# Retention projections of a hybrid decoder: seven products of quarter sums in place of eight

## The chip, the cores and the metric

The kernel runs on one core of a Trainium2 chip. The metric is the device time of one execution in microseconds (us). The kernel before took 1365.76 us, the median of two runs (1365.38 and 1366.14).

## The reference, cut to what matters

The model is a decoder trunk of four sub-layers on x of 512 tokens by 1024 features, float32: retention, a gated feed-forward block (ffn) with a short convolution, stick-breaking attention, and a second ffn. Each normalises its input and adds its output to x. Only the retention is changed:

```python
def _retention(h, w_in, w_out):              # h = rmsnorm(x, ret_norm), (B, S, D)
    proj = h @ w_in
    q, k, v, g = jnp.split(proj, [RET_QK, 2 * RET_QK, 2 * RET_QK + RET_V], axis=-1)
    ...                                       # rotary on q and k, per head
    scores = jnp.einsum('bhncd,bhnkd->bhnck', qc, kc) * dmat[None, :, None]
    intra = jnp.einsum('bhnck,bhnke->bhnce', scores, vc)
    ...                                       # a decayed state carries earlier blocks
    o = intra + jnp.moveaxis(cross, 0, 2)
    o = o * lax.rsqrt(jnp.mean(o * o, axis=-1, keepdims=True) + EPS)
    y = jax.nn.silu(g.astype(jnp.float32)) * o
    return y.astype(h.dtype) @ w_out
```

There are four heads; q and k have 256 columns a head, v and g 512. So a head has 512 columns of q and k, 512 of v, 512 of g, and 512 rows of the output projection.

## The kernel before

x lies feature-major in SBUF, eight tiles `x[0..7]` of 128 features by 512 tokens. A float32 product is made as three matmuls: each operand is split into a rounded high part and a low part (`split`, `parts`), and `mm3` (L137 to L139) issues high x high, high x low and low x high into one PSUM accumulator. x is split once as `xh`, `xl` (gain applied, but not the row factor r of the normalisation); weights arrive as chunks of 128x1024 (512 KB) through `chunk` (L122): SP issues the load into a `raw` buffer, ScalarE casts it to `hi` (L130), VectorE subtracts to get `lo` (L131). raw, hi and lo have five buffers each.

r is known only when all squares are summed (`rsqrt`, L216 to L220). It is applied late: to cos and sin, by which q and k are multiplied on their way out of PSUM (`rope`, L263 to L268); to v as a per-token scale (L111, L112, L304); to g by a multiplication on the way out (L367).

The retention goes head by head. `first4` computes q and k of head 0 while x is loaded. Each further projection step of a head (q and k, v, g) takes 96 matmuls of 512 columns, as does the output projection. `ret_scores` and `ret_av` are the causal attention with a fixed decay; `ret_av` keeps its four sums in PSUM until they are multiplied by their row factor (L357). PSUM has eight banks: four `att`, three `acc`, one `one`. The projections of heads 1 to 3 and all of g go through `acc`, attention through `att`. The output projection of head h-1 stands after v of head h, those of heads 2 and 3 at the end.

The order on each engine comes from the framework's planner: it takes the program's order as priority and its own estimate of when operands are ready, and lays out a fixed queue for each engine. So a later projection may be placed between the matmuls of attention.

In the ffn, four parts of the down projection are already made by seven products in place of eight (`fast_down`): both operands are cut into quarters, seven products of sums of quarters are made, and their results are added and subtracted into x. The sums of activations are made on VectorE (L434 to L436), the sums of weights by DMA from DRAM to DRAM on POOL's queue, with accumulation (`weight_sums`, L516, L518): 64 of them, started by an instruction on POOL (L500) that waits for r. Each sum needs up to six DMAs one after another, and two halves go side by side.

Of the kernel before, what the change touches and what calls it, by code (L numbers as in the profile page):

```python
# [9 lines left out]
F32 = mybir.dt.float32  # L10
F32R = mybir.dt.float32r
# [4 lines left out]
P = 128  # L16
# [15 lines left out]
HALF = S // 2  # L32
WARM = 4
# [3 lines left out]
class Kernel:  # L37
# [12 lines left out]
    def __init__(self, ctx, tc, t):  # L50
# [7 lines left out]
        self.pp = None  # L58
        self.att_pool()
        self.phase("ret")  # L60

# [4 lines left out]
    def phase(self, which):  # L66

        if self.pp is not None:
            self.pp.__exit__(None, None, None)
            self.pp = None  # L70
        if which:
            self.pp = self.tc.tile_pool(name=self.name(which), bufs=1, reuse_waits="tile")
            self.ph = self.pp.__enter__()

# [8 lines left out]
    BUFS = {"xh": 8, "xl": 8, "tt": 8, "rr": 2}  # L83
    PHASE = {"qk": 8, "vv": 8, "yy": 16, "pp": 8, "cs": 4, "ar": 2, "oh": 5, "ol": 5, "sq": 2, "sk": 4, "hl": 1, "bt": 2, "at": 2, "oo": 8}

    def sb(self, tag, cols=S, dt=F32):
        pool, bufs = (self.ap, self.BUFS) if tag in self.BUFS else (self.ph, self.PHASE)
        return pool.tile([P, cols], dt, tag=tag, bufs=bufs[tag], name=self.name(tag))

# [25 lines left out]
    def raw(self):  # L115
        return self.wp.tile([P, CH], F32, tag="raw", bufs=5, name=self.name("raw"))

    def chunk(self, c, cols=CH):

        nc = self.nc  # L120
        raw = self.raw()
        nc.sync.dma_start(raw[:, :cols], c)  # L122
        return self.parts(raw, cols)

    def parts(self, raw, cols=CH):
        nc = self.nc
        hi = self.wp.tile([P, CH], F32R, tag="hi", bufs=5, name=self.name("hi"))
        lo = self.wp.tile([P, CH], F32R, tag="lo", bufs=5, name=self.name("lo"))
        raw, hi, lo = raw[:, :cols], hi[:, :cols], lo[:, :cols]
# [15 lines left out]
    def first4(self, name, load=False):  # L145
# [3 lines left out]
        for k in range(KD):  # L149
            w = self.wchunk(name, k, S)  # L150
            if load:
                self.nc.sync.dma_start(self.x[k], self.t["xT"][k])
                self.norm_split(k, 0)
# [21 lines left out]
    def out_proj_steps(self, name, base, ys, last):  # L175

        n = len(ys)
        for c in range(4):
            w = self.wchunk(name, base + c, n * 256)
            for mm in range(2):  # L180
                ps = self.acc()
                for k in range(n):
                    s = slice(k * 256 + mm * P, k * 256 + mm * P + P)
                    self.mm3(ps, (w[0][:, s], w[1][:, s]), ys[k], k == 0, k == n - 1)
                    yield
                self.add_to_x(2 * c + mm, ps, last)

# [7 lines left out]
    def norm_split(self, m, which):  # L195
# [3 lines left out]
        self.xs.append(self.split(self.x[m], ("xh", "xl"), scale=g))  # L199
# [60 lines left out]
    def rope(self, p1, p2, tail):  # L260
        nc = self.nc
        a, b, e, f = (self.sb("tt") for _ in range(4))
        nc.vector.tensor_mul(a, p1, self.cos)  # L263
        nc.vector.tensor_mul(e, p1, self.sin)
        nc.vector.tensor_mul(b, p2, self.sin)
        nc.vector.tensor_mul(f, p2, self.cos)
# [7 lines left out]
    def ret_qk(self, h, ps):  # L274

        tail = self.sb("vv")
        tail = [tail[:, i * P : (i + 1) * P] for i in range(4)]
        out = []
        for i in range(2):
            c = 4 * (h - 1) + 2 * i  # L280
            x = ps[2 * i : 2 * i + 2] or [self.proj(self.wchunk("rqk", c + j), self.xs) for j in range(2)]
            out.append(self.rope(*x, tail[2 * i : 2 * i + 2]))
        return *out, tail

    def token_major(self, name, base):

        w = [self.wchunk(name, base + c) for c in range(4)]
        for i in range(NT):
# [5 lines left out]
            yield i, ps  # L294

    def ret_v(self, h):
        out = []
        for i, ps in self.token_major("rv", 4 * h):
            rc = self.rc[:, i : i + 1]
            if i < NT - 1:  # L300
                out.append(self.split(ps, ("vv", "vv"), scale=rc))
            else:
                out.append([self.sb("vv")])
                self.nc.scalar.activation(out[i][0], ps, AF.Copy, scale=rc)  # L304
        return out

    def ret_scores(self, h, q, k, tail):
        nc = self.nc
        dec = self.sb("cs", S + P)
# [24 lines left out]
    def ret_av(self, h, v, p):  # L334
# [3 lines left out]
        for m in range(4):  # L338
# [7 lines left out]
            os.append(o)  # L346
# [513 lines left out]
```

## Time and profile before

| what | value |
|---|---|
| median of two runs | 1365.76 us |
| profiled execution | 1366.12 us, span 1363.8 us |
| TensorE matmul busy | 1350.7 us, 99% of the span |
| VectorE, ScalarE busy | 991.1 us (73%), 599.0 us (44%) |
| DMA, mean over the span | 134 GB/s |

The profile is of one execution. The span runs from its first to its last instruction, and the execution's own time is 2.3 us more. A matmul's duration in the trace reaches over its successors, so what one costs is read from the distance between starts. "Busy" of the other engines is close to the time they can't be used by anybody else. The feed-forward's first matmul starts at 401.88 us, which is where the retention ends for TensorE.

### The profile page before, as it was taken

How to read it: one execution, taken by the hardware profiler on the slowest of the kernel's cores; microseconds unless marked ns; L12 is line 12 of the kernel's file. 1: busy time of each engine (PE TensorE's matmuls, PEld its weight loads, DVE VectorE, ACT ScalarE, POOL GpSimd, SP SyncE). 2: the span in 40 equal slices, each digit the busy share in tenths (PEclk: the TensorE clock that was granted, in tenths of full speed). 3: DMA queues.
4: the chain of work that ended last, by engine and by line, in shares of the span. 5: the costliest groups of instructions: out<-in, count | busy, mean ns of one | idle time of the engine just before them, and what ended most of it. 6: DMA issues, size and time to landing. Idle time of an engine off the chain costs nothing.

```text
span 1363.8 us, 18143 instructions
## 1 busy us (share of the span) xinstructions
PE 1350.7 (99%) x7016; PEld 1147.6 (84%) x7016; DVE 991.1 (73%) x1384; ACT 599.0 (44%) x844; POOL 78.3 (6%) x142
## 2 busy tenths in 40 slices
PE   9999999999999999999999999999999999999997
PEld 7888888888888889888988898787788899899887
DVE  7774564564768878688666668879799886787665
ACT  6443333333346444344344454444265443444434
POOL 1222220000000000000000021111000000000000
PEclk9999999999999999999999999999999999999999
DMA  8999992132224335433521574544143345235121
GB/s 299 305 290 243 301 239 96 47 108 77 62 77 141 99 102 169 126 93 107 183 82 55 165 183 124 130 118 109 39 145 95 108 127 168 77 113 174 55 70 62
DMA packets 58308, 182.77 MB, mean 134 GB/s; under 512 B 7024, under 2 KB 9200, under 8 KB 58224
## 3 DMA queue, kind: packets, MB, share of 16 engines
q1 hardware_dynamic: 42880, 136.25, 32.0%
q0 software_dynamic: 13824, 44.05, 13.3%
q10 hardware_dynamic: 1520, 1.33, 0.3%
q8 instruction: 55, 0.90, 0.3%
q14 instruction: 29, 0.24, 0.1%
HBM read 166.92 MB, written 33.55 MB: 147 GB/s over the span
## 4 chain that ended last, share of the span: by engine, by line
PE 95%; DVE 4%; issue 0%; ACT 0%; DVEq 0%; ACTq 0%
PE acc L138 23%; PE acc L137 23%; PE acc L139 23%; PE x L455 6%; PE att L137 4%; PE att L138 4%; PE att L139 4%; PE z L455 3%; PE acc L455 2%; PE one L626 1%; PE z L598 1%; DVE sg L603 1%; PE tp L618 1%; DVE at L620 1%; DVE bt L607 1%
## 5 line engine op out<-in xcount | busy, mean ns | idle before, releaser
L130 ACT CAST hi<-raw 128x1024 fp32r<-128x1024 f32 (+2 forms) x277 | 268.4, 969 | 428.8 <-PE acc L138 290.5
L138 PE MATMUL acc<-xl,hi 128*128 128x512 f32 x992 | 386.8, 390 | 0.0
L137 PE MATMUL acc<-xh,hi 128*128 128x512 f32 x992 | 386.5, 390 | 0.0
L139 PE MATMUL acc<-xh,lo 128*128 128x512 f32 x992 | 386.5, 390 | 0.0
L131 DVE TENSOR_TENSOR lo<-raw,hi 128x1024 fp32r<-128x1024 f32 (+2 forms) x277 | 309.3, 1118 | 61.3 <-ACT hi L130 59.6
L139 PEld LDWEIGHTS acc<-xh,lo 128*128 128x128 f32 x992 | 186.2, 188 | 38.5
L137 PEld LDWEIGHTS acc<-xh,hi 128*128 128x128 f32 x992 | 186.3, 188 | 38.1 <-DVE x L189 0.4
L138 PEld LDWEIGHTS acc<-xl,hi 128*128 128x128 f32 x992 | 186.3, 188 | 37.5 <-issue 0.2
L407 DVE SCALAR_TENSOR_TENSOR tt<-tt,vec,tt 128x511 f32<-128x511 f32 (+1 forms) x176 | 131.3, 747 | 4.0 <-ACT tt L405 1.4
L404 DVE TENSOR_TENSOR tt<-acc,rr 128x512 f32<-128x512 f32 x80 | 55.1, 688 | 75.6 <-PE acc L139 75.6
L189 DVE TENSOR_TENSOR x<-x,acc 128x512 f32<-128x512 f32 x72 | 48.9, 685 | 52.5 <-PE acc L139 52.4
L139 PE MATMUL acc<-hi,xl 128*128 128x512 f32 (+1 forms) x256 | 86.0, 336 | 0.0
L138 PE MATMUL acc<-lo,xh 128*128 128x512 f32 (+1 forms) x256 | 85.9, 336 | 0.0
L137 PE MATMUL acc<-hi,xh 128*128 128x512 f32 (+1 forms) x256 | 85.9, 336 | 0.0
L405 ACT ACTIVATE tt<-tt,vec 128x512 f32<-128x512 f32 x88 | 71.4, 812 | 11.3 <-DVE tt L404 10.2
L455 PE MATMUL x<-oh,hi 128*128 128x256 f32 x240 | 68.2, 284 | 0.0
L455 PE MATMUL x<-oh,lo 128*128 128x256 f32 x240 | 67.9, 283 | 0.0
L455 PE MATMUL x<-ol,hi 128*128 128x256 f32 x240 | 67.9, 283 | 0.0
L603 DVE TENSOR_TENSOR_SCAN sg<-sg,diag 128x512 f32<-128x512 f32 (+3 forms) x64 | 52.3, 818 | 2.0 <-ACT sg L600 1.2
L137 PEld LDWEIGHTS acc<-hi,xh 128*128 128x128 f32 x256 | 48.4, 189 | 5.3
L138 PEld LDWEIGHTS acc<-lo,xh 128*128 128x128 f32 x256 | 48.4, 189 | 5.3
L139 PEld LDWEIGHTS acc<-hi,xl 128*128 128x128 f32 x256 | 48.5, 189 | 4.9
(178 smaller groups left out, 2228.3 us busy)
## 6 DMA issues: line engine op xcount, KB each, us to landing
raw<-in_up SPq DMA_DIRECT2D x80, 512.0 KB, 4.1
sum<-in_fast POOLq DMA_DIRECT2D x36, 512.0 KB, 8.9
raw<-sum SPq DMA_DIRECT2D x24, 512.0 KB, 3.4
raw<-in_fast SPq DMA_DIRECT2D x18, 512.0 KB, 3.6
raw<-in_rv SPq DMA_DIRECT2D x16, 512.0 KB, 6.5
raw<-in_rg SPq DMA_DIRECT2D x16, 512.0 KB, 4.4
raw<-in_rout SPq DMA_DIRECT2D x16, 512.0 KB, 4.8
sk<-hl POOLq DMA_DIRECT2D x32, 256.0 KB, 4.4
```

The lines of the kernel that those rows point to most:

```text
L130: nc.scalar.copy(hi, raw)
L131: nc.vector.tensor_sub(lo, raw, hi.bitcast(F32))
L137: mm(out, a[0], b[0], start=start, stop=False)
L138: mm(out, a[0], b[1], start=False, stop=False)
L139: mm(out, a[1], b[0], start=False, stop=stop)
L189: self.nc.vector.tensor_add(self.x[m], self.x[m], ps)
L404: nc.vector.tensor_mul(u, ps, self.r)
L405: nc.scalar.activation(c, u, AF.Identity, scale=w[2], bias=w[3])
L407: nc.vector.scalar_tensor_tensor(c[:, i:], u[:, : S - i], w[2 - i], c[:, i:], op0=ALU.mult, op1=ALU.add)
L455: mm(out[:, :Q], a[ai], b[bi], start=start and k + i == 0, stop=k == nk - 1 and i == 2, skip_group_check=not start)
L598: nc.tensor.matmul(z[:, :nz], q[:, i * P : (i + 1) * P], k[:, :nz], start=m == 0, stop=m == 1)
L603: nc.vector.tensor_tensor_scan(sg[:, :n][:, ::-1], sg[:, :n][:, ::-1], self.diag[:, S - n :][:, ::-1], 0.0, op0=ALU.mult, op1=ALU.max,)
```

## The change

All of g, q and k of heads 1 to 3, and v of heads 1 to 3 are made by seven products in place of eight. q and k of head 0 (`first4`), v of head 0 (`ret_v0`), attention and the output projection keep their matmuls.

New operands: `ret_operands` makes, from x, gain and r, the normalised x and four sums of its quarters (features in pairs of tiles, tokens in halves), and splits them: four pairs `xo` of 128x1792. It stands after v of head 0. The sums of weights come from DMAs as in the ffn, in the order of `ORDER`: 10 new groups of eight DMAs, one chunk wide except the pair for v of heads 1 and 2, ahead of the ffn's. What starts them is now the last tile of x. The list of seven products is shared (`seven`); `feature_rows` makes feature-major results with 256 token columns a matmul (q and k, g, ffn), `token_rows` token-major ones for v, with 512 weight columns for heads 1 and 2 together and 256 for head 3.

A feature product uses the four `att` banks and two of `acc`; its results are gathered from PSUM into SBUF by ScalarE copies (first) and VectorE additions (later). `ret_av` copies its sums out of PSUM to SBUF. In the retention raw has three buffers, hi and lo four; after it each has five as before. The order of the steps is written out, with parts of the output projection between.

```diff
+ORDER = (
+    ("fg", 0, 1), ("fqk", 0, 1), ("fv", 0, 2), ("fg", 1, 1), ("fqk", 1, 1), ("fg", 2, 1), ("fqk", 2, 1),
+    ("fv3", 0, 1), ("fg", 3, 1), *((f"fast{l}_{s}", 0, 2) for l in range(2) for s in range(FAST[l])),
+)
...
-    BUFS = {"xh": 8, "xl": 8, "tt": 8, "rr": 2}
-    PHASE = {"qk": 8, "vv": 8, "yy": 16, "pp": 8, "cs": 4, "ar": 2, "oh": 5, "ol": 5, "sq": 2, "sk": 4, "hl": 1, "bt": 2, "at": 2, "oo": 8}
+    BUFS = {"tt": 8, "rr": 2}
+    OPERANDS = {"xh": 8, "xl": 8, "xo": 8}
+    PHASE = {"qk": 8, "vv": 6, "vr": 4, "tl": 1, "yy": 12, "pp": 7, "tr": 2, "dc": 1, "ar": 2, "oh": 5, "ol": 5,
+             "sq": 2, "sk": 4, "hl": 1, "bt": 2, "at": 2, "oo": 8, "sv": 8}
...
+    RING = {"raw": (3, 2), "hi": (4, 1), "lo": (4, 1)}
+    def ring(self, tag, dt):
+        a, b = self.RING[tag]
+        i = self.tiles[tag]
+        self.tiles[tag] = (i + 1) % (a if self.now == "ret" else a + b)
+        pool, tag, n = (self.wp, tag, a) if i < a else (self.ph, tag + "+", b)
+        return pool.tile([P, CH], dt, tag=tag, bufs=n, name=self.name(tag[:3]))
...
+    def seven(self, name, i, product, add, x, z, n=1):
+        w = [[self.t[name][c][q] for c in range(i, i + n)] for q in range(4)]
+        s1, s2, s3, s4 = ([self.sums[name][c][q] for c in range(i, i + n)] for q in range(4))
+        product(x, w[0], self.X11, True)
+        add(0, 0, x, 1, True)
+        product(z, s1, self.T1, True)
+        add(1, 1, z, -1, True)
+        product(x, s2, self.T2, False)
+        add(0, 1, x, 1, True)
+        y = [self.acc() for _ in range(2)]
+        product(y, w[1], self.X21, True)
+        add(0, 0, y, 1, False)
+        product(x, s3, self.T3, False)
+        add(1, 1, x, -1, False)
+        product(z, s4, self.X22, False)
+        add(0, 1, z, 1, False)
+        product(x, w[3], self.T4, False)
+        add(1, 0, x, -1, True)
+    def feature_rows(self, name, i, ops, x, z, add):
+        cols = 2 * len(ops) * P
+        def product(to, w, n, start):
+            w = self.chunk(w[0], cols)
+            for p in range(2):
+                self.quarter(to[p], w, p, ops, n, start)
+        self.seven(name, i, product, add, x, z)
+    def feature_tiles(self, name, i):
+        nc = self.nc
+        out = [self.sb("tt") for _ in range(4)]
+        def add(row, half, of, sign, first):
+            for p in range(2):
+                to = out[2 * p + row][:, half * Q : half * Q + Q]
+                if first:
+                    nc.scalar.activation(to, of[p][:, :Q], AF.Copy, scale=float(sign))
+                else:
+                    (nc.vector.tensor_add if sign > 0 else nc.vector.tensor_sub)(to, to, of[p][:, :Q])
+        x, z = ([self.att() for _ in range(2)] for _ in range(2))
+        self.feature_rows(name, i, self.ops, x, z, add)
+        return out
+    def token_rows(self, name, i, n, cols, out):
+        nc = self.nc
+        def product(to, w, q, start):
+            for c, chunk in enumerate(w):
+                w = self.chunk(chunk)
+                nk = CH // cols
+                for a in range(2):
+                    for k in range(nk):
+                        o = slice(q * Q + a * P, q * Q + a * P + P)
+                        op, b = [x[:, o] for x in self.ops[c * nk + k]], [x[:, k * cols : (k + 1) * cols] for x in w]
+                        for j, (ai, bi) in enumerate(((0, 0), (0, 1), (1, 0))):
+                            nc.tensor.matmul(
+                                to[a][:, :cols], op[ai], b[bi], start=start and c + k + j == 0,
+                                stop=c == n - 1 and k == nk - 1 and j == 2, skip_group_check=not start,
+                            )
+        def add(row, half, of, sign, first):
+            for a in range(2):
+                to, ps = out[row][2 * half + a], of[a][:, :cols]
+                if first:
+                    nc.scalar.activation(to, ps, AF.Copy, scale=float(sign))
+                else:
+                    (nc.vector.tensor_add if sign > 0 else nc.vector.tensor_sub)(to, to, ps)
+        x, z = ([self.att() for _ in range(2)] for _ in range(2))
+        self.seven(name, i, product, add, x, z, n)
+    def weight_sums(self):
+        nc, tc, t = self.nc, self.tc, self.t
+        self.sums = {n: {} for n in SUMS}
+        gate = nc.gpsimd.tensor_copy(self.gate, self.x[KD - 1][:, :1])
+        with tc.issue_after(getattr(gate, "ins", gate)):
+            for name, first, n in ORDER:
+                w, cs = t[name], range(first, first + n)
+                cols = w.shape[3]
+                d = {
+                    c: [
+                        self.dp.tile([P, cols + 16], F32, tag=f"{name}_{c}_{i}", bufs=1, name=self.name("sum"))[:, :cols]
+                        for i in range(4)
+                    ]
+                    for c in cs
+                }
+                self.sums[name].update(d)
+                s = lambda c, i: d[c][i]
+                for to, of in ((0, 2), (2, 0), (0, 3), (2, 2), (1, -1), (1, 0), (3, -2), (3, 1)):
+                    for c in cs:
+                        if (to, of) in ((0, 3), (2, 2), (1, 0), (3, 1)):
+                            nc.gpsimd.dma_start(s(c, to), w[c][of], accum_op=ALU.add)
+                        else:
+                            nc.gpsimd.dma_start(s(c, to), w[c][of] if of >= 0 else s(c, -1 - of))
...
+    def ret_operands(self):
+        nc, self.ops = self.nc, []
+        for j in range(KD // 2):
+            x = [self.sb("tt") for _ in range(4)]
+            for i in range(2):
+                k = 2 * j + i
+                nc.vector.scalar_tensor_tensor(x[i], self.x[k], self.vec[:, k : k + 1], self.r, op0=ALU.mult, op1=ALU.mult)
+            (x11, x12), (x21, x22), (t3, t1), (t2, t4) = ((a[:, :Q], a[:, Q:]) for a in x)
+            nc.vector.tensor_sub(t1, x11, x12)
+            nc.vector.tensor_sub(t3, x22, x12)
+            nc.vector.scalar_tensor_tensor(t2, t1, -1.0, x22, op0=ALU.mult, op1=ALU.subtract)
+            nc.vector.scalar_tensor_tensor(t4, t2, -1.0, x21, op0=ALU.mult, op1=ALU.subtract)
+            hi, lo = (self.sb("xo", 7 * Q, F32R) for _ in range(2))
+            for i, a in enumerate((x[2], x[3], x[1], x11)):
+                c = slice(2 * i * Q, min(2 * i + 2, 7) * Q)
+                nc.scalar.copy(hi[:, c], a)
+                nc.vector.tensor_sub(lo[:, c], a, hi[:, c].bitcast(F32))
+            self.ops.append((hi, lo))
...
-            os.append(o)
+            os.append(self.sb("yy"))
+            nc.scalar.copy(os[m], o)
...
-            ps = self.proj(self.wchunk("rg", 4 * h + m), self.xs)
...
+        for g, o in zip(self.feature_tiles("fg", h), os):
...
+        for x in (self.cos, self.sin):
+            first.append(self.sb("pp"))
+            nc.vector.tensor_mul(first[-1], x, self.r)
         self.weight_sums()
-        y = None
-        for h in range(RH):
-            q, k, tail = self.ret_qk(h, first if h == 0 else [])
-            v = self.ret_v(h)
-            if 0 < h < RH - 1:
-                self.out_proj("rout", 4 * (h - 1), y, None)
-            p = self.ret_scores(h, q, k, tail)
-            o = self.ret_av(h, v, p)
-            last, y = y, self.ret_y(h, o)
-        self.out_proj("rout", 4 * (RH - 2), last, None)
-        self.out_proj("rout", 4 * (RH - 1), y, 1)
+        def out_proj(steps, n):
+            for _ in range(8 * n):
+                next(steps, None)
+        def out_steps(h, y, last=None):
+            return self.out_proj_steps("rout", 4 * h, y, last)
+        qk = self.ret_qk(0, first)
+        v = self.ret_v0()
+        self.ret_operands()
+        y = self.ret_y(0, self.ret_av(v, self.ret_scores(0, *qk)))
+        qk = self.ret_qk(1, None)
+        steps = out_steps(0, y)
+        out_proj(steps, 2)
+        v = [[self.sb(tag) for tag in tags] for tags in (("pp", "pp", "pp", "yy"), ("vr",) * NT)]
+        self.token_rows("fv", 0, 2, S, v)
+        v1 = self.ret_split(v[0])
+        out_proj(steps, 2)
+        y = self.ret_y(1, self.ret_av(v1, self.ret_scores(1, *qk)))
+        steps = out_steps(1, y)
+        out_proj(steps, 1)
+        qk = self.ret_qk(2, None)
+        out_proj(steps, 3)
+        v1 = self.ret_split(v[1])
+        y = self.ret_y(2, self.ret_av(v1, self.ret_scores(2, *qk)))
+        steps = out_steps(2, y)
+        out_proj(steps, 1)
+        qk = self.ret_qk(3, None)
+        out_proj(steps, 1)
+        v = [self.sb("vr") for _ in range(NT)]
+        self.token_rows("fv3", 0, 1, HALF, [[x[:, r * HALF : (r + 1) * HALF] for x in v] for r in range(2)])
+        v1 = self.ret_split(v)
+        out_proj(steps, 1)
+        y = self.ret_y(3, self.ret_av(v1, self.ret_scores(3, *qk)))
+        out_proj(steps, 1)
+        self.operands()
+        for _ in out_steps(3, y, 1):
+            pass
```

## Rows read from the trace of the kernel before

**Rows 1.** Page: busy us of engines; DMA busy tenths in 40 slices.
```profile
PE 1350.7 (99%) x7016; PEld 1147.6 (84%) x7016; DVE 991.1 (73%) x1384; ACT 599.0 (44%) x844; POOL 78.3 (6%) x142
...
DMA  8999992132224335433521574544143345235121
```

**Rows 2.** Timeline of PE, two steady stretches: start us, us, operation.
```profile
479.90 0.39 PE L137 MATMUL acc<-xh,hi 128*128 128x512 f32 x1
...
510.95 0.39 PE L139 MATMUL acc<-xh,lo 128*128 128x512 f32 x1
...
511.29 0.28 PE L455 MATMUL x<-ol,hi 128*128 128x256 f32 x1
...
517.53 0.28 PE L455 MATMUL x<-oh,lo 128*128 128x256 f32 x1
```

**Rows 3.** Windows: us, busy by engine (x instructions), PEclk, DMA share, GB/s.
```profile
28.40:50.40 22.00, 22.00 (x99) 18.21 (x98) 20.43 (x31) 9.14 (x15) 8.13 (x12) 1.00 0.91 243
...
100.00:200.00 100.00, 100.00 (x459) 83.44 (x458) 56.62 (x73) 36.14 (x48) 25.73 (x37) 1.00 0.98 266
...
513.00:529.00 16.00, 16.00 (x136) 16.00 (x135) 15.40 (x25) 7.27 (x7) 0.00 (x0) 1.00 0.48 147
```

**Rows 4.** Timeline of PE in attention of head 0.
```profile
50.39 0.39 PE L137 MATMUL att<-qk,qk 128*128 128x512 f32 x1
...
53.89 0.47 PE L137 MATMUL att<-pp,vv 128*128 128x512 f32 x1
...
54.20 0.40 PE L137 MATMUL acc<-xh,hi 128*128 128x512 f32 x1
...
61.52 0.39 PE L345 MATMUL att<-pp,vv 128*128 128x128 f32 x2
```

**Rows 5.** Timeline of DVE: the reciprocal for r, and rope of head 0.
```profile
27.65 3.35 DVE L220 RECIPROCAL rr<-tt 128x512 f32<-128x512 f32 x1
...
35.19 0.68 DVE L264 TENSOR_TENSOR tt<-att,cs 128x512 f32<-128x512 f32 x1
...
35.79 0.68 DVE L265 TENSOR_TENSOR tt<-att,cs 128x512 f32<-128x512 f32 x1
```

**Rows 6.** Groups by form, 0 to 450 us: busy us, mean ns, idle.
```profile
L131 DVE TENSOR_TENSOR lo<-raw,hi 128x1024 fp32r<-128x1024 f32 x69 | 84.0, 1219 | 14.9 <-ACT hi L130 13.8
...
L130 ACT CAST hi<-raw 128x1024 fp32r<-128x1024 f32 x69 | 72.7, 1054 | 120.0 <-PE acc L138 98.2 <-PE att L138 8.8 <-issue 7.0
...
L112 DVE SCALAR_TENSOR_TENSOR xl<-x,vec,xh 128x512 fp32r<-128x512 f32 x16 | 12.0, 750 | 4.4 <-ACT xh L111 4.4
...
L330 DVE TENSOR_TENSOR pp<-tt,pp 128x384 fp32r<-128x384 f32 x4 | 2.2, 555 | 0.5 <-ACT pp L329 0.5
...
L330 DVE TENSOR_TENSOR pp<-tt,pp 128x256 fp32r<-128x256 f32 x4 | 1.7, 420 | 0.0
...
L329 ACT CAST pp<-tt 128x512 fp32r<-128x512 f32 x4 | 2.5, 620 | 4.7 <-DVE tt L327 4.7
```

**Rows 7.** DMA, 0 to 220 us: queues (packets, MB, share), issues (us to landing).
```profile
q0 software_dynamic: 8704, 31.46, 58.1%
...
q1 hardware_dynamic: 8784, 26.14, 32.6%
...
sum<-in_fast POOLq DMA_DIRECT2D x36, 512.0 KB, 8.9
...
raw<-in_rv SPq DMA_DIRECT2D x12, 512.0 KB, 7.0
```

**Rows 8.** Timeline of SP and POOL: last x load, first and last sums.
```profile
9.40 0.43 SPq L152 DMA_DIRECT2D x<-in_xT  x1
...
32.05 2.23 POOL L518 DMA_DIRECT2D sum<-in_fast  x4
...
198.06 0.83 POOL L516 DMA_DIRECT2D sum<-in_fast  x1 [3.31 <-DMA sum<-sum]
```

**Rows 9.** Windows, the span's last 4 us, columns as in rows 3.
```profile
1360.00:1364.00 4.00, 0.00 (x0) 0.00 (x0) 0.10 (x1) 0.00 (x0) 0.00 (x0) 0.50 0.56 197
```

More of the change, by code (lines that the diff above doesn't have):

```diff
@@ L257, in setup @@
         )
-    def rope(self, p1, p2, tail):
-        nc = self.nc
[L262 to L266, printed above, removed]
+    T3, T1, T2, T4, X21, X22, X11 = range(7)
+    def seven(self, name, i, product, add, x, z, n=1):
[16 more added lines that the diff above has]
+        add(1, 0, x, -1, True)
@@ L267, in rope @@
+    def rope(self, p1, p2, cos, sin, tail, own=False):
+        nc = self.nc
+        a, e, b = (self.sb("tt") for _ in range(3))
+        f = p2 if own else self.sb("tt")
+        nc.vector.tensor_mul(a, p1, cos)
+        nc.vector.tensor_mul(e, p1, sin)
+        nc.vector.tensor_mul(b, p2, sin)
+        nc.vector.tensor_mul(f, p2, cos)
         nc.vector.tensor_sub(a, a, b)
@@ L272, in rope, with ret_qk, ret_v0 @@
         return out
[L274 to L276 removed]
+    def ret_qk(self, h, first):
+        tail = self.sb("tl")
         tail = [tail[:, i * P : (i + 1) * P] for i in range(4)]
[L278 to L287, printed above, removed]
+        cos, sin = (self.cos, self.sin) if h else first[4:]
+        x = first[:4] if h == 0 else self.feature_tiles("fqk", h - 1)
+        return *(self.rope(*x[2 * i : 2 * i + 2], cos, sin, tail[2 * i : 2 * i + 2], h > 0) for i in range(2)), tail
+    def ret_v0(self):
+        w = [self.wchunk("rv", c) for c in range(4)]
+        out, rc = [], self.token_major_r()
         for i in range(NT):
@@ L458, in fast_down, with add @@
     def fast_down(self, l, s, ops, half):
-        nc, t = self.nc, self.t[f"fast{l}_{s}"][half]
-        cols = 2 * len(ops) * P
-        w11, w12, w22 = t[0], t[1], t[3]
-        s1, s2, s3, s4 = (d[half] for d in self.sums[l, s])
-        first, second = slice(0, Q), slice(Q, S)
-        x = [self.psum("x", 2) for _ in range(2)]
-        z = [self.psum("z", 2) for _ in range(2)]
-        def product(to, w, n, start=False):
-            w = self.chunk(w, cols)
+        nc = self.nc
+        def add(row, half_t, of, sign, first):
@@ L471, in product @@
             for p in range(2):
-                self.quarter(to[p], w, p, ops, n, start)
-        def add(row, tokens, of, sign=1):
-            for p in range(2):
-                x = self.x[4 * half + 2 * p + row][:, tokens]
+                x = self.x[4 * half + 2 * p + row][:, half_t * Q : half_t * Q + Q]
                 (nc.vector.tensor_add if sign > 0 else nc.vector.tensor_sub)(x, x, of[p][:, :Q])
-        product(x, w11, self.X11, True)
-        add(0, first, x)
-        product(z, s1, self.T1, True)
@@ L520, in ffn @@
+        x, z = ([self.psum(tag, 2) for _ in range(2)] for tag in "xz")
+        self.feature_rows(f"fast{l}_{s}", half, ops, x, z, add)
     def ffn(self, l, last):
```

127 lines of the change are left out of this document (47 added, 80 removed).

## Prediction

> **What bounds the kernel now.** I read the page's engine table and slices first. TensorE is busy in 1350.7 us of the 1363.8 us span, and the DMA engines are nearly full in the first 200 us and not later [rows 1]. Then I took its instruction starts: of 138 matmuls of 512 columns the first starts at 479.90 and the last at 510.95, so one costs 31.05 / 137 = 0.2267 us; of 53 matmuls of 256 columns the first starts at 511.29 and the last at 517.53, so one costs 6.24 / 52 = 0.120 us [rows 2]. They stand back to back, so a removed matmul gives its spacing back, as long as nobody makes TensorE wait instead. Then I read the retention by stretches [rows 3]: TensorE has no gap at a granted clock of 1.00, VectorE is busy in 20.4 of 22.0 us just after the first projection and in 57% later, and the DMA share is 0.98 from 100 to 200 us. The profiled execution took 1366.12 us, 0.36 us above the median 1365.76; the sum is made against it.
>
> **Matmuls.** Each projection step of one head has 4 tiles x 8 x 3 = 96 matmuls of 512. Removed: q and k of three heads, g of four, v of three, 10 x 96 = 960, at 0.2267 = 217.6 us. Added: a feature-major seven product has 7 x 2 x 4 x 3 = 168 matmuls of 256; there are 4 (g) + 3 (q, k) + 1 (v of head 3, also 256 wide) = 8, so 1344 at 0.120 = 161.3 us. v of heads 1 and 2 together is 7 x 2 x 2 x 2 x 3 = 168 of 512, 38.1 us. Net: 217.6 - 199.4 = **18.3 us given back**, all on the path [rows 1, 2]. In columns alone it would be one eighth; the 256-wide product costs 53% of a 512-wide one and eats a third of that.
>
> The Trainium skill ("TensorE: Matmul & The Clock Gate", section "Back-to-back issue gap") puts the spacing at N/2.4 + 2.5 ns, that is 109 and 216 ns; an estimate by it would give back 24 us. The measured spacings are longer, so they decide.
>
> **Operands, the large new cost.** The seven products need sums of quarters of the normalised x, and these need r. VectorE finishes its reciprocal at 27.65 + 3.35 = 31.0 us [rows 5]. Consecutive 128x512 operations start 0.60 us apart (35.19, 35.79), some 0.09 us under their duration; so I take 0.60 for a 512 (0.66 for the scalar_tensor_tensor), 0.33 for a 256, 0.46 for a 384 and 1.13 for a weight chunk's low part [rows 5, 6]. From 31.0 VectorE has, for head 0: the last chunk of v 1.1; cos and sin 1.2; rope, 12 + 4 low parts at 0.60 = 9.6; the token-major r 1.4; three low parts of v 2.0; and, new, per pair of k tiles two scalar_tensor_tensor of 512, four operations of 256, three low parts of 512 and one of 256, four times: 8 x 0.66 + 16 x 0.33 + 12 x 0.60 + 4 x 0.33 = **19.1 us**. Together 34.4, so the operands are ready at 65.4. Every product runs over all four pairs within its first 12 matmuls, so g of head 0 can't begin before. Before, g read xh and xl, which existed, and ran into attention's waits. Now TensorE has v until 50.4 and attention until 61.7, 11.0 us without the matmuls of g between [rows 4], so until 61.4, and then nothing: out-projection 0 needs y, q and k of head 1 need the same operands. Low end: attention's own VectorE work (scores 3.0, squares 2.4) and one chunk of g (1.1) fit in between, g at 65.4 + 6.5 = 71.9, a stall of 10.5. High end: the operands are written ahead of the scores and go first, the first low part of the scores stands at 65.4 + 1.8 = 67.2, attention's second part (53.89 to 61.66, 7.8 us [rows 4]) follows, g at 75.0, a stall of 13.6. I take **13**, near the high end, since the operands come first in the program.
>
> In the last 4 us, without a matmul, TensorE's granted clock is 0.50, the 1.2 GHz level [rows 9]. So a stall this long can leave half clock behind it: nothing at best, at worst the 7.8 us of attention twice. I take **1.5**. No row times the rise.
>
> **Attention without filler.** Before, matmuls of g stand between those of scores and of probabilities times v, one already 0.3 us after the first [rows 4]. g now needs the same four PSUM banks as attention, so it can't. Heads 1 to 3 wait for probabilities (0.60 + ACT 0.62 + 0.60 = 1.8 [rows 5, 6]) less what the later scores cover: 0 to 2 us each; I take 1, together **3**. Here also lies rope (9.6 us) beside out-projection's adds, on three accumulation banks.
>
> **Off the path.** Chunks split go from 40 to 70: 30 x 1.13 = 34 us more on VectorE, 30 x 1.05 = 32 on ACT [rows 6]. Per head VectorE then has 25 chunks 28.3, rope 9.6, evictions 5.8, adds to x 4.8, v 1.8, scores 3.0, attention's sum, reciprocal and products 8.1, y 4.8: 66 us beside 20.2 (g) + 20.2 (q, k) + 19.0 (v) + 21.8 (out) + 11.0 = 92 us of TensorE. That is hidden. ACT's quarter evictions and four PSUM copies a head hide likewise; they read a bank that is written again a product (2.9 us) later.
>
> **DMA.** Up to 220 us the software queue moved 31.46 MB in 58.1% of 220 us, 4.06 us of all engines per MB, the loads 2.74 us per MB [rows 7]. Added sums: 10 groups x 8 x 0.524 MB = 42 MB, 170 us; added chunks 15.7 MB, 43 us. Per head that makes 3 groups x 17.0 + 25 chunks x 1.44 = 87 us of DMA in 92 us. The sums now start when the last tile of x is there (issued at 9.40, which I take as ready at 16), not at 32 [rows 8]. With loads at 0.39 of the engines a group takes 17.0 / 0.58 = 29 us, so group k is ready near 16 + 29 k: 45 for g of head 0 (wanted from 72), 306 for the last (wanted by 365). The tightest want 34 to 35 us a group. POOL's and SP's queues wait for each other only there. A product feeds on 0.524 MB in 24 x 0.120 = 2.9 us, with three raw buffers in place of five; four split chunks stand ahead, so I book **1.5** us, between 0 and the third rival.
>
> **Sum.** 1366.1 - 18.3 + 13 + 1.5 + 3 + 1.5 = 1366.8, less 0.4 to the median: **1366 us**, no change. With all low ends 1358, with a long stall, doubled attention and 2 us a head 1376.
>
> **Rivals.**
> First, the stall at head 0 is mostly covered, because VectorE's list is shorter or is ordered better than I have it: 1366.1 - 18.3 + 2 to 7 = 1350 to 1356. For it: VectorE's gaps before 50 us are small but exist; against it: the 34 us list and its start at 31.0 rest on rows [rows 5]. It also holds the case where I over-booked waits. 0.17.
>
> Second, slower: the weight sums come late. A group now has one chunk (v of heads 1 and 2 two), so its eight DMAs form a chain of six dependent steps (copy, add, copy, add, copy, add) on POOL's queue, and SP's queue stands behind a load that waits for them. Before, two halves shared each step, 64 DMAs from 32 to 199 us, 21 us per eight [rows 8]. It decides above 35 us a group. At the median landing of 8.9 us [rows 7] a step, less a copy issued early, 6 x 8 = 48 us: the last sum stands at 16 + 8 x 48 + 2 x 29 = 458 against 365, some 90 us late, 1366 + 90 = 1456. At 40 us it would be 51 late by the same working with ten groups, 1417. Against it: that median holds three or four DMAs in flight, a lone chain meets only the loads. 0.14.
>
> The Trainium skill ("DMA: Bandwidth & Descriptors", section "Anatomy of one DMA — SWDGE (gpsimd) path") fits one such DMA with 2.0 us plus bytes over 436 GB/s, 3.2 us here; by that estimate a chain takes 19 us and is never late. No row shows a lone chain.
>
> Third, the loads run short: with three raw buffers and 7.0 us to landing (v's chunks up to 220 us [rows 7]) plus 2.7 for split and issue, a chunk arrives every 3.2 us against 2.9; at 9 us every 3.9, 25 of them 98 us against 92, 6 us a head, 1366 + 6 x 3.3 = 1386. For it: DMA at 87 of 92 us; against: the same products in the feed-forward show TensorE full at DMA share 0.48 [rows 3]. 0.16.
>
> **How the numbers follow.** My forecast, 1356 to 1378: 0.50; covered stall 0.17; short loads, 1378 to 1393: 0.16; late sums 0.14; something that gives back more than the matmuls: 0.03. About 2%, 27 us, is what a measurement of this kernel can tell from no change. The matmuls give 18.3 at the most, so faster by over 2% gets 0.03; slower takes the late sums and a little of the short loads, 0.17; within 2%, 0.80. The range 1351 to 1393 leaves out the late sums and the lowest edge.
>
> **What would show it.** A TensorE gap of 10 to 14 us between 50 and 76 us, ended by VectorE's xo; matmuls at 0.120 in the products; g of head 0 starting at 72 to 75; the retention's end within 10 us of its old place. The forecast is wrong if that gap is under 7 us, if POOL waits for sums show as TensorE gaps after 100 us, or if waits on raw recur in each head.

## The result: 5% slower, and the profile after

The changed kernel takes 1436.93 us (two runs, 1433.54 and 1440.32) against 1365.76 us: a ratio of 1.052, 95% interval 1.041 to 1.063. The forecast was 1366 us, no change. The profiled execution is the one of 1440.32 us, with a span of 1438.5 us.

The page of the changed kernel, as in [rows 1]: busy time of TensorE with its instructions, and the DMA engines' busy tenths in 40 slices of 36 us.

```profile
PE 1371.4 (95%) x7568; PEld 1173.7 (82%) x7568; DVE 1054.5 (73%) x1492; ACT 660.8 (46%) x975; POOL 131.8 (9%) x222
...
DMA  9999999999983433633341175444214336226121
```

TensorE is no longer busy all the time (95%, 99% before), and the DMA engines are full for eleven slices, to about 400 us, where they were full for five.

Stretches of the changed kernel (us, busy us of PE, PEld, DVE, ACT and POOL with instructions, granted TensorE clock, DMA share, GB/s), to be read against [rows 3].

```profile
50.00:100.00 50.00, 32.33 (x188) 30.07 (x187) 38.06 (x63) 24.50 (x42) 13.71 (x21) 0.76 1.00 284
100.00:200.00 100.00, 89.13 (x479) 74.83 (x477) 58.26 (x75) 43.87 (x64) 22.54 (x34) 0.97 1.04 314
350.00:400.00 50.00, 41.48 (x275) 38.34 (x273) 32.41 (x46) 20.79 (x34) 11.76 (x18) 0.97 1.03 301
513.00:529.00 16.00, 16.00 (x70) 12.83 (x70) 12.12 (x14) 7.56 (x9) 0.00 (x0) 1.00 0.30 97
```

From 100 to 200 us TensorE had no gap; now it has 11 us of them, and 8.5 us from 350 to 400. After 458 us it is full again.

TensorE's timeline in the changed kernel (start, us, operation; in brackets the wait before it and what ended it): around the gap at head 0, at the first weights of its g, at one of the later gaps, at the first matmul of the feed-forward, and the ends of a run of 57 matmuls.

```profile
55.23 0.61 PE L465 MATMUL att<-tl 128*128 128x128 f32 x4
69.23 1.22 PE L156 MATMUL att<-pp,vv 128*128 128x512 f32 x2 [13.40 <-ACT pp L476]
...
81.56 0.28 PE L623 MATMUL att<-xo,lo 128*128 128x256 f32 x1
86.11 0.80 PE L237 MATMUL one<-tt,ones 128*128 128x512 f32 x1 [4.27 <-ACT tt L137]
...
143.38 0.80 PE L156 MATMUL acc<-yy,hi 128*128 128x512 f32 x1 [5.56 <-DVE x L210]
...
458.49 0.40 PE L156 MATMUL att<-xh,hi 128*128 128x512 f32 x1
...
499.70 0.40 PE L156 MATMUL acc<-xh,hi 128*128 128x512 f32 x1
...
512.82 0.40 PE L158 MATMUL acc<-xh,lo 128*128 128x512 f32 x1
```

The gap before 86.11 us is named after ACT's tt, but ACT itself had stood waiting for the first weights of g:

```profile
81.68 1.04 ACT L149 CAST hi<-raw 128x1024 fp32r<-128x1024 f32 x1 [4.83 <-DMA raw<-in_fg]
```

This gives two separate losses.

**Inside the retention, 56.6 us.** The feed-forward starts at 458.49 us, 401.88 before. The waits in front of TensorE's rows up to there add up to 53.8 us, none before. Matmuls that ran slower than the spacings of [rows 2] cost some 20 us more than before. So -18.3 + 53.8 + 20 = 55.5 us.

**After the retention, 18.1 us.** From there to the end it takes 1438.5 - 458.5 = 980.0 us against 1363.8 - 401.9 = 961.9, though the change touches no product there. The last two rows show it: 13.12 / 56 = 0.2343 us a matmul, 0.2267 in [rows 2]. The 512-wide matmuls that stream xh or xl have it, 2592 of them by the trace (the expectations below count 2496): 2592 x 0.0076 = 20 us. xh and xl have moved from the left end of SBUF to the right.

The supply of weights: the DMA of 0 to 440 us (queues: packets, MB, share of the engines; issues: count, size, median us to landing), which answers [rows 7].

```profile
q0 software_dynamic: 20224, 73.41, 65.5%
q1 hardware_dynamic: 16501, 53.84, 32.9%
...
raw<-sum SPq DMA_DIRECT2D x40, 512.0 KB, 8.1
...
raw<-in_rout SPq DMA_DIRECT2D x16, 512.0 KB, 7.5
```

POOL's timeline, the first sum, the last of the retention and the last of the feed-forward, for [rows 8].

```profile
16.95 1.22 POOL L387 DMA_DIRECT2D sum<-in_fg  x2
...
246.89 0.86 POOL L385 DMA_DIRECT2D sum<-in_fg  x1 [4.85 <-DMA sum<-sum]
...
416.12 0.82 POOL L385 DMA_DIRECT2D sum<-in_fast  x1 [1.55 <-DMA sum<-sum]
```

The retention's ten groups take (246.9 - 17.0) / 10 = 23 us each on average, under the 35 that would have made them late. But the feed-forward's sums now run until 416 us; they were issued by 198 before.

The chain of waits in the changed kernel (start, us, what) shows how TensorE starves: a chunk lands, ACT splits it, VectorE writes its low part, and only then is a raw buffer free for the next load.

```profile
160.22 9.00 DMA raw<-sum
...
169.32 1.05 ACT hi L149
...
170.40 1.24 DVE lo L150
171.66 6.70 DMA raw<-sum
...
178.46 1.06 ACT hi L149
179.54 1.24 DVE lo L150
180.80 7.67 DMA raw<-in_rout
```

One buffer needs some 8.2 + 1.06 + 1.24 us for a chunk; three together bring one every 3.5 us, and a seven product wants one every 24 x 0.120 = 2.9.

### The profile page after: what moved, and what is told of

Read it like the earlier page. It is cut to its first block, busy times and chain, and to the rows that moved or that the text cites. A ratio compares the mean times of both kernels' runs of the same rounds, so it can differ in the third digit from the quotient of the medians.

```text
span 1438.5 us, 19682 instructions
## 1 busy us (share of the span) xinstructions
PE 1371.4 (95%) x7568; PEld 1173.7 (82%) x7568; DVE 1054.5 (73%) x1492; ACT 660.8 (46%) x975; POOL 131.8 (9%) x222
## 4 chain that ended last, share of the span: by engine, by line
PE 72%; DMA 11%; DVE 11%; ACT 4%; issue 2%; SPq 0%; DVEq 0%; ACTq 0%
PE acc L156 16%; PE acc L157 16%; PE acc L158 16%; PE x L623 6%; DMA raw<-sum 5%; PE z L623 3%; DVE lo L150 3%; PE att L156 3%; PE att L157 3%; PE att L158 3%; PE att L623 2%; DMA raw<-in_rout 2%; ACT hi L149 2%; PE acc L623 2%; DMA raw<-in_fqk 2%
## 5 line engine op out<-in xcount | busy, mean ns | idle before, releaser
L157 PE MATMUL acc<-xl,hi 128*128 128x512 f32 x608 | 241.1, 397 | 0.0
L158 PE MATMUL acc<-xh,lo 128*128 128x512 f32 x608 | 241.0, 396 | 0.0
L156 PE MATMUL acc<-xh,hi 128*128 128x512 f32 x608 | 241.0, 396 | 0.0
L158 PEld LDWEIGHTS acc<-xh,lo 128*128 128x128 f32 x608 | 114.5, 188 | 27.8
L157 PEld LDWEIGHTS acc<-xl,hi 128*128 128x128 f32 x608 | 114.5, 188 | 26.7 <-issue 0.2
L156 PEld LDWEIGHTS acc<-xh,hi 128*128 128x128 f32 x608 | 114.5, 188 | 26.5
L623 PE MATMUL att<-xo,hi 128*128 128x256 f32 x672 | 125.2, 286 | 4.9 <-DVE tt L327 2.6
L623 PEld LDWEIGHTS att<-xo,hi 128*128 128x128 f32 x672 | 106.0, 192 | 7.0 <-DVE tt L327 3.2
L623 PE MATMUL att<-xo,lo 128*128 128x256 f32 x336 | 95.6, 285 | 0.4 <-DVE lo L150 0.4
L623 PEld LDWEIGHTS att<-xo,lo 128*128 128x128 f32 x336 | 64.4, 192 | 1.3 <-DVE lo L150 0.8
```

What stands on the lines that cost most here:

```text
L156: mm(out, a[0], b[0], start=start, stop=False)
L157: mm(out, a[0], b[1], start=False, stop=False)
L158: mm(out, a[1], b[0], start=False, stop=stop)
L623: mm(out[:, :Q], a[ai], b[bi], start=start and k + i == 0, stop=k == nk - 1 and i == 2, skip_group_check=not start)
```

## The experiments

### Pad of 32 bytes under xh and xl

The changed kernel with a pad at the right, and the kernel before with one at each end of the pool of xh and xl:

```
+ pad = tile_pool("pad", side="right"); pad.tile([P, 8], F32)      # after: xh, xl, xo down by 32 bytes
+ pad0 before pool "ap", pad1 behind it: [P, 8] F32 each           # before: xh, xl, rr, tt up by 32 bytes, all later pools by 64
```

> The changed kernel with one 32-byte pad at the end of SBUF, so that xh, xl and xo begin at multiples of 64 bytes (in the changed kernel they begin 32 bytes past one; in the kernel before at one). Placement theory: each of the 2496 matmuls that stream xh or xl after the retention goes from 0.234 back to 0.227 us, 2496 x 0.0076 = 19 us, total 1437 - 19 = 1418. Rival, that the spacing comes from traffic or from the order of the instructions: spacing stays at 0.234, total 1437 +- 7.

> The kernel before with xh and xl alone moved by 32 bytes, so that they begin 32 bytes past a multiple of 64; nothing else changes. Placement theory: 3264 matmuls stream xh or xl (768 in the retention, 2496 after it), each 0.0076 us longer: 1366 + 25 = 1391, and the spacing reads 0.234. Rival, that the placement does nothing: 1366.

Measured: 1435.58 us (ratio 1.051, 1.0493 to 1.0528) and 1385.28 us (1.0143, 1.0128 to 1.0158). A multiple of 64 is not the rule: in the changed kernel the spacing went from 0.2343 to 0.2325 us only. But the shift made the kernel before 19.7 us slower, with 0.2333 us for matmuls that stream xh or xl. It moved more than was meant: yy, oh and ol lie behind both pads and went up by 64 bytes, and by the trace their 512-wide matmuls went from 0.2267 to 0.229 us and their 256-wide ones from 0.120 to 0.118. So places of operands alone are worth as much as was lost after the retention, by a rule still unknown then; xh and xl alone were not isolated here.

### Trains of matmuls at chosen places

```
+ for s, m in ((0, 0), (0, 16), (0, 32), ..., (160, 160), (320, 480), (320, 448), ...):
+     72 x matmul(acc, big[s + k*512 or s + 20480 + k*512], big[45056 + m + k*2048 (+ 16384)])
```

> This kernel leaves the whole computation out and measures one thing: trains of 72 matmuls of 512 columns (hi by xh, hi by xl, lo by xh, over eight k and three banks, as a projection has them) on one large tile, with the stationary pieces at s bytes and the moving pieces at m bytes behind a multiple of 512, first with the other engines idle, then with loads and splits of chunks beside them. In the kernel before, stationary and moving pieces lie at the same place modulo 512 (320 and 320) and a matmul costs 0.2267 us; after the change they lie at 320 and 480 (0.2343); with 32 bytes of pad at 320 and 448 (0.2325); with the kernel before shifted at 320 and 352 (0.2333). If their distance modulo 512 decides, every train with s = m costs 0.226 to 0.228 and the others 0.231 to 0.236. If only the place of the moving piece itself decides, s = m = 32 is as slow as s = 0, m = 32. If it needs other engines' traffic, all trains of the first part cost the same and only the second part tells them apart. If none of these, all cost the same in both parts, and the place is not the cause.

TensorE's timeline, the first matmul of some trains of 72. The trains that start there, as (s, m): (0, 0), (0, 16), (0, 32); (160, 160), (256, 256); (320, 480), (320, 448), (320, 352). They follow each other without a gap, so the start of the next one ends a train.

```profile
53.54 0.39 PE L904 MATMUL acc<-big 128*128 128x512 f32 x1
...
69.86 0.39 PE L904 MATMUL acc<-big 128*128 128x512 f32 x1
...
86.54 0.40 PE L904 MATMUL acc<-big 128*128 128x512 f32 x1
...
403.03 0.39 PE L904 MATMUL acc<-big 128*128 128x512 f32 x1
...
419.38 0.40 PE L904 MATMUL acc<-big 128*128 128x512 f32 x1
...
518.78 0.39 PE L904 MATMUL acc<-big 128*128 128x512 f32 x1
...
535.65 0.39 PE L904 MATMUL acc<-big 128*128 128x512 f32 x1
...
552.38 0.39 PE L904 MATMUL acc<-big 128*128 128x512 f32 x1
```

Distance 0 costs (69.86 - 53.54) / 72 = 0.2267 us, distance 16 (86.54 - 69.86) / 72 = 0.2317. With both operands at 160 it is (419.38 - 403.03) / 72 = 0.2271: the place itself does not matter. At 320 and 480, as in the changed kernel, it is (535.65 - 518.78) / 72 = 0.2343; at 320 and 448, as with 32 bytes of pad, 0.2324. The other trains: 32 and 96 bytes apart 0.2333 and 0.2335, 64 apart 0.2289, 128 apart 0.2333 or 0.2324, 160 apart 0.2342, 192 and 224 apart 0.2334 and 0.2333, and 256 apart 0.2271 again. (Where the moving piece lies 64 below the stationary one, which is 192 above it modulo 256, it is 0.2332.) 57344 bytes further away the same distances cost the same, and so they do beside loads and splits (0.2333 at 32, 0.2342 at 160, 0.2269 with both at 160). What decides is the distance of the moving from the stationary piece modulo 256 bytes. In the kernel before, hi starts at byte 42304 of a partition and xh at 83264, a distance of 160 x 256; after the change they start at 34112 and 196576, 634 x 256 + 160. The pad made that 128 and the shift of the kernel before made it 32, and each spacing measured there is that of its train.

### xh, xl and xo at the weights' place

```
+ pad = tile_pool("pad", side="right"); pad.tile([P, 40], F32)     # 160 bytes
```

> The changed kernel with 160 bytes of pad at the right end, so that xh, xl and xo lie at 320 modulo 512 as the weights' hi and lo do. If the distance modulo 512 decides, a 512-wide matmul with xh or xl costs 0.2267 us again and 2496 x 0.0076 = 19 us come back: 1417 to 1420 us. Rival: the place has another rule, or it is the distance in the large (xh now far above the weights), and the time stays at 1433 to 1437 us.

Measured 1418.21 us (ratio 1.0359, 1.0342 to 1.0376), as expected. Two matmuls from a run of 82 of this kernel's timeline:

```profile
511.63 0.39 PE L158 MATMUL acc<-xh,hi 128*128 128x512 f32 x1
...
529.99 0.39 PE L158 MATMUL acc<-xh,hi 128*128 128x512 f32 x1
```

18.36 / 81 = 0.2267 us. The feed-forward starts at 462.17 of 1424.5 us, so what follows takes 962.3 us, 980.0 without the pad and 961.9 before the change. This explains the loss after the retention but for 0.4 us. The total is less firm than this stretch: six runs lie between 1412.6 and 1426.3 us.

### No sums

```
- self.sums[name].update(d)
+ self.sums[name].update({c: [w[c][i] for i in range(4)] for c in cs}); continue
```

> The changed kernel without the sums of weights: their DMAs are left out, and the products load quarters of the weights in their place, with the same loads otherwise. Supply theory (loads share the DMA engines with the sums, and three raw buffers can't cover it): waits on loads end, TensorE's gaps after head 0 shrink from some 40 us to under 10, the 13 us gap of head 0 stays, total 1437 - 40 to 50 = 1387 to 1397. Rival (VectorE and the order of the queues make the gaps): total not below 1427.

Measured 1381.36 us, 6 us under the range expected; an estimate with xh and xl in place is 1362 (less 19). A stretch of it, and a row of its timeline:

```profile
100.00:200.00 100.00, 99.12 (x557) 86.37 (x557) 68.70 (x85) 53.17 (x79) 0.00 (x0) 1.00 0.47 151
```

```profile
67.03 1.22 PE L156 MATMUL att<-pp,vv 128*128 128x512 f32 x2 [13.40 <-ACT pp L477]
...
399.64 0.40 PE L156 MATMUL att<-xh,hi 128*128 128x512 f32 x1
```

The DMA share falls to 0.47, raw<-in_rout lands in 3.7 us in place of 7.5, and only the gap of head 0 and one of 0.9 us are left. The second row is the feed-forward's first matmul. The seven products themselves, with their splits, quarter evictions and bank reuse, make no gaps.

### Light operands, and then five raw buffers

```
- hi, lo = (self.sb("xo", 7 * Q, F32R) for _ in range(2))
+ hi = self.sb("xo", 7 * Q, F32R); self.ops.append((hi, hi))    # and no tensor_sub for lo
- RING = {"raw": (3, 2), ...}
+ RING = {"raw": (5, 0), ...}                                    # second kernel only, in the room of lo
```

> The changed kernel without the low parts of the summed operands: 16 VectorE subtractions (8.5 us) are left out and the products use the high part twice. VectorE theory of head 0: the gap between scores and probabilities times v goes from 13.4 to about 5 us, and with less time at half clock the total falls by 9 to 14, to 1423 to 1428. Rival (the loads bound head 0 as well): the gap moves behind, to g of head 0, and the total stays within 4 us, 1433 or more.

> Against the run with light operands (1421.9 us; it leaves out the same sixteen low parts, and its time is read against that run alone): five raw buffers in the retention in place of three. If what starves TensorE is the latency of a chunk with three buffers (landing 8.5 us plus split 2.4 us, so a chunk every 3.6 us where a product wants one every 2.9), five buffers bring a chunk every 2.2 us: of the 34 us of idle TensorE after head 0 most goes, and the time is 1385 to 1400. If the DMA engines themselves are full (share 1.0 to 400 us), more loads in flight only land later, and the time stays at 1417 to 1425 with the landing of raw<-sum above 11 us.

Measured 1421.87 and 1375.10 us. The first is 1 us under its range; in it the gap of head 0 shrank, as a row of its timeline shows:

```profile
60.64 1.22 PE L156 MATMUL att<-pp,vv 128*128 128x512 f32 x2 [4.77 <-ACT pp L475]
```

13.4 - 4.8 = 8.6 us for 12 low parts of 0.60 us and 4 of 0.33, 8.5: VectorE's list does set that gap. The second, 46.8 us faster, went beyond the lower end expected. The DMA engines were just as full (share 1.03 from 250 to 350 us), a load of a sum took longer to land (11.6 us from 100 to 400 us), and TensorE had 2 us of gaps after head 0.

### Five raw buffers in the changed kernel

```
- RING = {"raw": (3, 2), "hi": (4, 1), "lo": (4, 1)}
+ RING = {"raw": (5, 0), "hi": (3, 2), "lo": (3, 2)}
  # head 0: the fourth chunk of v has hi and lo where xo is written later
```

> The changed kernel with five raw buffers and three hi and lo during the retention in place of three and four (the fourth chunk of v of head 0 has its hi and lo in the room that the operands take later); same sums, same operands, same places. In the run with light operands five raw buffers took 46.8 us off, and the idle TensorE after head 0 went from 34 to 3 us. If too few loads in flight is the cause in the changed kernel as well, 42 to 52 us go and the time is 1385 to 1395, with the gap at head 0 still 13 to 14 us. Rival: that run gained by its room or its lighter VectorE; then VectorE's queue (adds to x behind late low parts) keeps most gaps and the time stays above 1415 us.

Measured 1389.41 us (ratio 1.0172, 1.0158 to 1.0186): 47.5 us less. The gap at head 0 is 2.3 us longer than in the changed kernel: loads now run ahead, and two chunks' low parts of 1.22 us stand among the operands on VectorE, at 51.86 and 53.34 us, where there were none. Its stretch, its gap at head 0, and its low parts from 72 to 440 us (busy us, mean ns, idle before them and its cause):

```profile
100.00:200.00 100.00, 98.53 (x545) 85.08 (x544) 68.02 (x88) 52.92 (x78) 21.15 (x31) 1.00 1.05 323
```

```profile
69.90 1.22 PE L156 MATMUL att<-pp,vv 128*128 128x512 f32 x2 [15.69 <-ACT pp L481]
```

```profile
L150 DVE TENSOR_TENSOR lo<-raw,hi 128x1024 fp32r<-128x1024 f32 (+1 forms) x95 | 111.0, 1174 | 46.8 <-ACT hi L149 44.5 <-PE one L237 2.1
```

In the changed kernel the same group, in the same stretch, reads:

```profile
L150 DVE TENSOR_TENSOR lo<-raw,hi 128x1024 fp32r<-128x1024 f32 x86 | 104.6, 1223 | 99.7 <-ACT hi L149 99.6
```

At the same DMA share (1.03 from 72 to 400 us in both kernels) VectorE waits half as long for chunks. A load of a sum takes 11.0 us to land there, 8.2 before, but five buffers at (11.0 + 2.3) / 5 can bring a chunk every 2.7 us and three at (8.2 + 2.3) / 3 every 3.5. This kernel has fewer hi and lo buffers than the changed one, so the gain comes from raw.

### The feed-forward's sums later

```
- self.weight_sums()
+ self.weight_sums(self.x[KD - 1], ORDER[:-4])     # at the old place
+ self.weight_sums(self.x[0], ORDER[-4:])          # behind the last out-projection
```

> The changed kernel with the four groups of sums of the feed-forward started when the last out-projection has written x, not behind the retention's groups. If the sums' traffic beside the loads makes the gaps, the stretch from 250 to 450 us loses its 20 us of idle TensorE and most of the 12 us at half clock: 1408 to 1416 us, with DMA share under 0.8 there; the retention still ends some 28 us later than in the kernel before. Rival: the gaps after 250 us come from VectorE's queue or from three raw buffers alone; then the time stays at 1430 to 1440 us. Should the late sums stall the feed-forward, gaps of TensorE stand at 550 to 620 us.

Measured 1410.98 us (two runs, 1406.83 and 1415.13; ratio 1.033, 1.0294 to 1.0366), as expected. A stretch of it:

```profile
250.00:300.00 50.00, 49.94 (x326) 45.95 (x325) 36.79 (x51) 25.38 (x42) 0.00 (x0) 1.00 0.38 125
```

So fewer sums beside the loads and more loads in flight cure the same gaps. The feed-forward starts at 425.08 us, and what follows takes 979.9 us: the sums cost nothing there.

### All together, and a filler for head 0

```
+ five raw buffers; 160 bytes of pad; sums of the feed-forward late         # first kernel
+ ps = self.ret_g0()       # second: four chunks, eight products of xh and xl, between v and attention
+ self.ret_operands()      # then the operands; g <- ps * r behind them
+ self.token_rows("fv", ...); out_proj(steps, 4)   # third: v of heads 1, 2 first; sums not late
```

> The run with five raw buffers, and also 160 bytes of pad (xh, xl and xo at the weights' place modulo 512) and the feed-forward's sums after the retention. The pad gives 18 to 19 us after the retention by the earlier run; with the gaps already gone the late sums give 0 to 4. So 1362 to 1374 us, within 1% of the kernel before. Rival: the two are not additive, since sums late in the feed-forward now meet its loads with the same five buffers: 1380 or more.

> As the run before it, and g of head 0 as eight products of the un-normalised xh and xl, between v of head 0 and its attention, so that TensorE has 22 us of work while VectorE writes the operands. If the gap of 13.7 us at head 0 is the operands' lateness and the half clock behind it costs 2 to 4 us more, less 1.6 us that the eight products cost over the seven: 14 to 17 us off the run before, 1347 to 1358 us, under the 1365.5 us of the kernel before. Rival: the gap only moves, to the q and k of head 1 or to the scores behind g's evictions; then the time is within 4 us of the run before.

> The run with g of head 0 as eight products (1371.5 us), with two orders changed: the sums of the feed-forward again behind the retention's, and v of heads 1 and 2 ahead of out-projection 0 in place of between its halves. In that run TensorE still has gaps of 7 us at 101 to 124 us, where out-projection 0 waits for y of head 0 and for VectorE's adds to x, and of 2.3 us at 426 to 429, where the late sums start. If out-projection only came too early for VectorE, v's 38 us of products cover it: 7 + 2 us, and some half clock, go, 1360 to 1364 us, which would be under the 1365.8 us of the kernel before. Rival: the sums of v are then wanted 13 us sooner and come late, or VectorE's backlog stands elsewhere: 1368 to 1376 us.

Measured 1374.15 us (ratio 1.0061, 1.0046 to 1.0077), 1371.50 (1.0038, 1.0025 to 1.0050) and 1365.39 (0.9993, 0.9984 to 1.0002). The first came out just above what was expected. The second gave 2.7 of the expected 14 to 17 us: its rival was right. Two of its stretches:

```profile
50.00:75.00 25.00, 25.00 (x112) 20.72 (x111) 24.75 (x44) 17.55 (x27) 5.17 (x8) 1.00 1.04 298
...
100.00:125.00 25.00, 18.49 (x95) 15.15 (x95) 23.66 (x38) 10.22 (x18) 5.97 (x9) 0.90 1.00 257
```

TensorE is full from 50 to 75 us, where it had done 9.3 us of work in the run before, but VectorE, busy 24.75 of 25 us there, hands on its backlog, and from 100 to 125 us TensorE waits for it. (That this backlog is the operands' is argued from VectorE's full stretches; no run takes them off this kernel.) The third kernel gave back 6.1 us more, short of the 1360 to 1364 us expected, and ends level with the kernel before, not ahead of it; 3.5 us of the gap stand at 104.77 us, behind a quarter's eviction on VectorE:

```profile
104.77 1.19 PE L646 MATMUL att<-xo,hi 128*128 128x256 f32 x4 [3.49 <-DVE tt L329]
```

## Why the prediction was wrong

**Matmuls, -18.3 us: right** in the retention. The run without sums has its feed-forward at 399.64 us: 401.9 - 18.3 + 13.4 + 0.9 (its only other gap) is 397.9; the 2 us left have room for the half clock behind that gap.

**Operands, 13 us: right**, 13.4 us, with attention's second part at 69.23 behind VectorE's list, as the high end of the prediction has it (67.2 there), and 8.6 us less when 8.5 us are taken off that list. So the wait's row names ACT's pp, and not xo as the prediction's sign had it.

**Sums late, 0.14: refuted**, 23 us a group against the 35 from which it decides. The Trainium skill's figures ("DMA: Bandwidth & Descriptors", section "Anatomy of one DMA — SWDGE (gpsimd) path") gave an estimate of 19 us for such a chain; the trace has 23 from one group to the next.

**DMA: this step failed.** The term "I book 1.5 us, between 0 and the third rival" measured 47.5 us with the half clock behind its gaps, by the run that changes only the buffers; the third rival had the mechanism, priced 20 us and given 0.16. Three things in its working were wrong. It held against the rival that the same products run full in the feed-forward, in a stretch at DMA share 0.48, while the retention's DMAs were counted at 87 of 92 us; at share 1.04 a load takes twice as long to land, 8.1 us against the 3.5 to 4.4 of the run without sums. It compared averages over a head, 25 chunks against 92 us: the need comes in bursts of seven chunks at 2.9 us each, and three raw and four split buffers can store little of the time in which attention wants no chunk (this last is argued from the buffers, not measured alone). And it stopped at the retention's own sums, though the feed-forward's four groups follow them in the same queue until 416 us; taken out of the way they give 26 us (1436.9 to 1411.0, each a median of two runs 7 to 8 us apart).

**Half clock, 1.5 us: about right for the stall that it was booked for, too small for the kernel.** At head 0 attention's second part took 9.9 us (69.23 until the first matmul of g, at 79.10) in place of 7.8, 2 us more, and so g began later than the 72 to 75 of the forecast's signs. But matmuls slower than nominal cost 20 us more than before up to the retention's end, because the later gaps bring half clock too. The stretches behind the gap before 143.38 us:

```profile
143.00:147.00 4.00, 3.62 (x9) 2.91 (x10) 3.86 (x6) 0.69 (x2) 0.08 (x1) 0.54 1.01 241
147.00:151.00 4.00, 4.00 (x19) 3.23 (x18) 2.96 (x3) 1.05 (x1) 1.36 (x2) 1.00 1.06 288
```

A granted clock of 0.54 is 1.2 GHz for nearly all of the four us. Behind the wait of 2.0 us before 201.16 us it is 0.57 from 201 to 205; such waits are paid twice in part. With the gaps most of the slow matmuls went too.

**Attention without filler, 3 us: nothing.** With five raw buffers the only gap behind probabilities is head 0's; the changed kernel has two more, of 2.5 and 3.8 us before 296.25 and 401.70 us, which went with the other gaps.

**Not in the sum at all: 18 us after the retention.** The diff moves xh and xl to a pool on the right, and the prediction has no term for that. The pad of 160 bytes gives it back: 17.7 us after the retention, 18.7 in the medians.

Together: -18.3 + 13.4 + 47.5 (gaps and their half clock) + 18.7 = 61.3 of the 71.2 us; the head 0 gap's own half clock and the few gaps that five buffers leave (5 us of waits, and some 5 us of slow matmuls in the run with five buffers) are the rest.

## What to carry to other kernels

Before a change that adds transfers, work out how often the buffers in flight can deliver at the landing time of a full DMA, and compare it with the need inside a burst: landing plus split, over the number of raw buffers. A DMA share of 1 was not yet the bound here; two more buffers took 47 us off at the same share. When a diff moves a matmul operand to another pool, compare its address with the stationary one's, modulo 256 bytes. And a filler that hides the first wait for an operand does not make the operand free: here VectorE's 19 us at a busy time seem to come back as a wait of TensorE some 50 us later.

## What the runs showed of the hardware

A 512-wide fp32r matmul costs 0.2267 to 0.2274 us when the moving and the stationary piece lie a multiple of 256 bytes apart, 0.2289 when the moving one lies 64 above such a multiple, and 0.232 to 0.234 at 16, 32, 96, 128, 160, 192 and 224 (trains above): at 160 that is 3% more for each such matmul, by an address. Places in the rest of SBUF, one distance larger by 57344 bytes, and other engines' loads and splits changed it by 0.0007 us at most (0.0009 at 128).

For 256-wide matmuls no train was run, but the kernels show that they do not follow this. The first and the last of 145 matmuls of a product, in the run with five raw buffers (xo 160 bytes off) and in the one that adds the pad (a multiple of 256 apart):

```profile
224.10 0.28 PE L628 MATMUL att<-xo,lo 128*128 128x256 f32 x1
...
241.20 0.28 PE L628 MATMUL att<-xo,lo 128*128 128x256 f32 x1
```

```profile
223.86 0.28 PE L631 MATMUL att<-xo,lo 128*128 128x256 f32 x1
...
241.13 0.28 PE L631 MATMUL att<-xo,lo 128*128 128x256 f32 x1
```

That is 17.10 / 144 = 0.1188 us off the multiple and 17.27 / 144 = 0.1199 on it. So the address that costs a 512-wide matmul 3% saves a 256-wide one 1%. Why is open.

The Trainium skill ("DMA: Bandwidth & Descriptors", section "Queues, rings and completion order") says that a DMA engine takes its queues in turn, a packet at a time. The changed kernel and the run with five raw buffers fit that, though they don't prove it: with five loads waiting in place of three SP's queue moved 43.72 MB from 72 to 400 us in place of 40.83, while POOL's queue, which in both had packets under way in all but 3 to 4 of the 328 us, moved 58.53 MB in place of 59.01.
